# A hybrid layer's last attention pair: two pooling blocks in separate buffers, at other places of a hand-written order

## The chip, the cores and the metric

The kernel runs on one core of a Trainium2 chip. Its time is device microseconds of one execution. Five engines work side by side, each through its own queue in order: TensorE (PE: matmuls, with weight loads listed as PEld), VectorE (DVE), ScalarE (ACT), GpSimd (POOL) and SyncE (SP), which here issues the DMAs.

## What is computed

The reference is one layer over a sequence of 1024 rows of 1024 channels, in float32:

```
h = RMSNorm(x)
[pool_v | pool_gate | sb_q | sb_k | sb_v | sb_gate | mem_q | mem_gate] = h @ W_in
A (256 channels, 4 groups of 64): causal means over windows of 2, 4, 8, 16 rows, minus the row itself,
   times a 64x64 matrix per group, times a scale per channel
B (8 heads of 64): causal stick-breaking attention (sigmoid breaks, cumulative products, no softmax)
C (4 heads of 64): softmax attention into 256 memory tokens, with RMSNorm of q and k
each group's output * SiLU(its gate); concatenated @ W_out; + x
```

The change concerns group A. In the reference it is

```
csum  = cumsum(u) with a zero row ahead
means = (csum[t+1] - csum[max(t+1-w, 0)]) / count        # w = 2, 4, 8, 16 for the four groups
y     = einsum('bsgc,gcd->bsgd', stack(means) - u, pool_w) * pool_scale * SiLU(pool_gate)
```

## The kernel before

Activations lie with channels on the 128 partitions and the 1024 rows along the free axis. A float32 operand of a product is split into a high and a low part, and each product is three matmuls (high x high, high x low, low x high). A projection unit (`Unit`) makes 128 columns of `h @ W_in` for all rows: 16 steps of three matmuls, eight for the first 512 rows (th = 0) and eight for the rest, each half into one PSUM bank of the tag pj, of which there are two. Behind a half comes its `evac`: for a gate a sigmoid on ScalarE (L413) and a multiply on VectorE (L416), for a value of the pooling a copy on ScalarE (L893). Four quarters of the next unit's weights are split on ScalarE (L277) and GpSimd (L278) while a unit runs.

The attention of group B runs in four pairs of heads. Each pair has its q tiles in qa0, qb0 (even pairs) or qa1, qb1 (odd), its k tiles in KA0, KB0 or KA1, KB1, and its v tile in V0 or V1. The last pair, number 3, has the odd set. Its work goes in chunks: scores z on TensorE (L754), a sigmoid into a tile be on ScalarE (L760), a scan of up to 1024 elements on VectorE (L769); then, for one head of the pair, transposes on TensorE (ta, L593), a high part on ScalarE (L597) and a low part on VectorE (L598); for the other head a 32x32 transpose on VectorE (L771), a store to DRAM and a load back (zd; L779, L799 to L805), a high part on ScalarE (L824) and a low part on GpSimd (L825). Then come the products with v (av, L611), and their end on ScalarE (L630) and VectorE (L633, L634).

`weave` lays the attention's steps of a pair and a list of fill steps into one order, by planned TensorE times. For the last pair the fill is five units, 80 steps: u_pv[1], u_gp[1], u_gp[0], u_pv[0], u_gm[0] (the value and gate of pooling block 1, the gate and value of block 0, and a memory gate). The dictionary `places` puts further steps behind a fill step's number. `soon(us, fn)` puts work off until that much planned time has passed. In this part the order of all engines' instructions is the order of the program; behind `hand.close()` a planner orders VectorE, ScalarE, GpSimd and SyncE again, and may set transfers of the last part (`load_b`, L1228) earlier.

Group A is done by `pool_parts(r, gg)`, once for each block r of 128 channels (two groups of 64 channels). Its steps in order:

- `weights`: a memset on GpSimd (L902), two loads of pool_w by SyncE (L905), and later a split on ScalarE and GpSimd (L908, L909);
- `window_add(n, c)`: sums of two neighbours, then four, and so on, on VectorE (L927), 8 for block 1 and 4 for block 0, with short copies of the first columns on ScalarE (L931);
- `mean(h, c)`: four for each block, on VectorE (L941, L942 for the first 16 columns, L944), then, put off by 3.3 and 4.4 us of planned time, a high part ph on ScalarE (L949) and a low part pl on GpSimd (L952);
- `out_step(th)`: three matmuls into py (L969 to L971) and, soon after, the scale and the gate on VectorE (L974).

Both blocks use the same tiles: KA0 for the values and sums (us), V0 for pl, qa0 for the second sum (ps2), qb0 for ph, and the tag vt for the matrices (pw). Behind the 80 steps the second memory gate u_gm[1] runs (u_mg in the profile, as u_gm[0]), and then the output projection as seven block products in place of eight (oA, oS; L1274 to L1276) with operands of w_out loaded into qa0 with qb0, KA0, KB1.

Of the kernel before, what the change touches and what calls it, by code (L numbers as in the profile page):

```python
# [10 lines left out]
F32R = mybir.dt.float32r  # L11
# [5 lines left out]
P = 128  # L17
# [10 lines left out]
def layer_kernel(  # L28
# [17 lines left out]
    pool = ctx.enter_context(tc.tile_pool(name="pool", bufs=1))  # L46
# [9 lines left out]
    def f(ap):  # L56
        return ap.bitcast(F32)
# [3 lines left out]
    def ps(tag, name):  # L61
        return psum.tile([P, 512], F32, tag=tag, name=name, bufs=banks[tag])
# [9 lines left out]
    def slot(tag, name, dt=F32):  # L72
        return pool.tile([P, 1024], dt, tag=tag, name=name, bufs=bufs.get(tag, 1))

    def slot2(tag, name, dt=F32):
        return pool.tile([P, 2048], dt, tag=tag, name=name)
# [103 lines left out]
    def run(steps):  # L180
        for us, fn in steps:
            fn()
            tick(us)
# [23 lines left out]
    def tick(us):  # L207
        clock[0] += us
        while pending and pending[0][0] <= clock[0]:
            heapq.heappop(pending)[2].run()  # L210
# [5 lines left out]
    def weave(main, fill, keep=0, lag=0.0):  # L216
        span = sum(s.pe for s in main) + sum(c for c, _ in fill[: len(fill) - keep])
        total = sum(s.occ + s.pe for s in main)
        now, chain_end, gone, n = 0.0, lag, 0.0, 0
        ready = {}  # L220
        for s in main:
            at_ = max([span * gone / total] + [ready.get(k, 0.0) for k in s.needs])
            while n < len(fill) and now < at_:
                now += fill[n][0]
                fill[n][1]()
                tick(fill[n][0])
                n += 1
            s.fn()
            tick(s.pe)
            now = max(now, at_) + s.pe  # L230
            gone += s.occ + s.pe
            chain_end = max(chain_end, now) + s.occ
            for g in s.gives:
                ready[g] = chain_end + s.lat
        run(fill[n:])
# [50 lines left out]
    def chain(units, after=None):  # L286
        steps = []
        for n, u in enumerate(units):
            nxt = units[n + 1] if n + 1 < len(units) else after
            a = list(u.steps)  # L290
            if nxt is not None:
                a[0] = (KC, lambda f0=a[0][1], nxt=nxt: (f0(), nxt.load()))
                for i in range(4):
                    k = 7 + 2 * i
                    a[k] = (KC, lambda f0=a[k][1], nxt=nxt, i=i: (f0(), nxt.quarter(i)))
            steps += a
        return steps

    def lazy(make):
        box = []  # L300

        def get():
            if not box:
                box.append(make())
            return box[0]

        return get
# [577 lines left out]

    def pool_parts(r, gg):
        wbox = []
        get = lazy(lambda: slot2("KA0", f"us{r}"))
        pl_get = lazy(lambda: slot2("V0", f"pl{r}", dt=F32R)[:, 0:1024])
        box = []  # L890

        def evac(th, c, pt):
            nc.scalar.activation(get()[:, c], pt[:], AF.Copy)  # L893

        halves = (slice(0, 512), slice(512, 1024))

        def weights():
            t = pool.tile([P, 513], F32R, tag="vt", name=f"pw{r}")
            s2 = slot("qa0", f"ps2{r}")
            bw, bwr = s2[:, 896:1024], t[:, 0 : 2 * P].rearrange("p (n c) -> p n c", n=2)  # L900
            wbox.append(bwr)
            nc.gpsimd.memset(bw, 0.0)  # L902
            for h in range(2):
                rows = slice(h * HD, (h + 1) * HD)
                nc.sync.dma_start(bw[rows, rows], pool_w[0, 2 * r + h])  # L905

            def split():
                nc.scalar.activation(bwr[:, 0, :], bw, AF.Copy)  # L908
                nc.gpsimd.tensor_tensor(bwr[:, 1, :], bw, f(bwr[:, 0, :]), op=ALU.subtract)  # L909

            todo.append(soon(4.5, split))
            u, s = get()[:, 0:1024], get()[:, 1024:2048]
            box.extend([u, s, s2, slot("qb0", f"ph{r}", dt=F32R)])

        todo, heads = [], []

        def window_add(n, c):
            u, s, s2 = box[:3]
            if n == 1:
                todo[0].run()  # L920
            step = 1 << n
            prev, cur = (u if n == 0 else (s, s2)[(n - 1) % 2]), (s, s2)[n % 2]
            lo = HD if n == 2 * r + 1 else 0
            c0 = max(c.start, step)
            if c.start == 0 and n > 0:
                heads[-1].run()
            nc.vector.tensor_tensor(  # L927
                cur[lo:P, c0 : c.stop], prev[lo:P, c0 : c.stop], prev[lo:P, c0 - step : c.stop - step], op=ALU.add
            )
            if c.start == 0:  # L930
                heads.append(soon(2.0, lambda: nc.scalar.activation(cur[lo:P, 0:step], prev[lo:P, 0:step], AF.Copy)))  # L931

        def mean(h, c):
            (u, s, s2, ph), pl = box, pl_get()
            n = 2 * r + h
            heads[-1].run()
            rows = slice(h * HD, (h + 1) * HD)
            src, dst = (s, s2)[n % 2], (s, s2)[(n + 1) % 2]
            cn = cnt[rows, r * 16 : r * 16 + 16]
            if c.start == 0:  # L940
                nc.vector.tensor_tensor(dst[rows, 0:16], src[rows, 0:16], cn, op=ALU.mult)  # L941
                nc.vector.tensor_tensor(dst[rows, 0:16], dst[rows, 0:16], u[rows, 0:16], op=ALU.subtract)  # L942
            d = slice(max(16, c.start), c.stop)
            nc.vector.scalar_tensor_tensor(  # L944
                dst[rows, d], src[rows, d], cn[:, 15:16], u[rows, d], op0=ALU.mult, op1=ALU.subtract
            )

            def high():
                nc.scalar.activation(ph[rows, c], dst[rows, c], AF.Copy)  # L949

            def low():
                nc.gpsimd.tensor_tensor(pl[rows, c], dst[rows, c], f(ph[rows, c]), op=ALU.subtract)  # L952

            todo.append(soon(3.3, high))
            todo.append(soon(4.4, low))

        mix = [(0.0, weights)]
        mix += [(0.0, lambda n=n, c=c: window_add(n, c)) for n in range(2 * r + 2) for c in halves]
        mix += [(0.0, lambda h=h, c=c: mean(h, c)) for c in halves for h in range(2)]

        def out_step(th):
            ph, pl = box[3], pl_get()
            bwr = wbox[0]
            for it in todo:
                it.run()
            g = gg()
            c = slice(th * 512, (th + 1) * 512)
            pt = ps("pj", f"py{r}_{th}")
            nc.tensor.matmul(pt[:], bwr[:, 0, :], ph[:, c], start=True, stop=False)  # L969
            nc.tensor.matmul(pt[:], bwr[:, 0, :], pl[:, c], start=False, stop=False)  # L970
            nc.tensor.matmul(pt[:], bwr[:, 1, :], ph[:, c], start=False, stop=True)  # L971
            soon(
                0.5,
                lambda: nc.vector.scalar_tensor_tensor(  # L974
                    g[:, c], pt[:], gcol[:, 16 + r : 17 + r], g[:, c], op0=ALU.mult, op1=ALU.mult
                ),
            )

        return Unit(r * P, f"pv{r}", evac), mix + [(KC, lambda th=th: out_step(th)) for th in range(2)]
# [99 lines left out]
    u_q, u_k, u_v, u_g = [[sb[p][i][-1] for p in range(4)] for i in range(4)]  # L1079
# [84 lines left out]
    attn = sb_slots()  # L1164
# [3 lines left out]
    gp, u_gp = zip(*[gate_unit(256 + r * P, f"pg{r}", lambda r=r: gp_get()[:, r * 1024 : (r + 1) * 1024]) for r in range(2)])  # L1168
    gm, u_gm = zip(*[gate_unit(2816 + pr * P, f"mg{pr}", "be", lambda pr=pr: y_back[pr], (("pj", "pj"), ("tr", "av"))[pr]) for pr in range(2)])
    u_pv, po = zip(*[pool_parts(r, gp[r]) for r in range(2)])  # L1170
    weave(attn[2], chain([u_q[3], u_k[3], u_g[3], u_v[3]], u_pv[1]))
    units = chain([u_pv[1], u_gp[1], u_gp[0], u_pv[0], u_gm[0]], u_gm[1])

    places = {}
    for r, lo, hi, outs in ((1, 18, 46, (53, 57)), (0, 64.5, 77.5, (79.5, 79.7))):
        todo = po[r][:-2]
        for n, st in enumerate(todo):
            places.setdefault(int(lo + n * (hi - lo) / len(todo)), []).append(st)
        for at_, st in zip(outs, po[r][-2:]):
            places.setdefault(int(at_), []).append(st)  # L1180
# [213 lines left out]
```

## Time and profile before

| | |
|---|---|
| median of 3 runs | 527.57 us (525.86 to 528.05) |
| the profiled execution | 528.35 us, its span 526.2 us, mean clock 0.983 |
| TensorE busy | 499.3 us (95%) |
| VectorE busy | 403.4 us (77%) |
| ScalarE, GpSimd busy | 300.6 and 248.2 us |

The profile's times are from the span's start. A row of the timeline has start, length, engine, line, operation, output<-inputs by the program's names without numbers (so pv is u_pv[0] or u_pv[1]), and in brackets the idle time before it with what ended it. A row of the waits has who waited for whom, us in total, times, and the longest. A row of the table by stage has the stretch, its length, the busy time and number of instructions of each engine, the mean granted clock of TensorE (1.00 is full), the share of DMA and GB/s. The end of a matmul is modelled, so two matmuls overlap in the list; the time from start to start is what one occupies.

### The profile page before, as it was taken

To read this page: it belongs to the slowest core of one execution; us is meant where nothing else is said; L and a number is where in the kernel's file an instruction comes from. 1 tells how busy PE (TensorE), PEld (TensorE's weight loads), DVE (VectorE), ACT (ScalarE), POOL (GpSimd) and SP (SyncE) were. 2 spreads that over 40 slices of the span, in tenths; PEclk is the share of its full clock that TensorE was granted. 3 is DMA by queue.
4 is the path that set the end of the run, shared out by engine and by line. 5 is a ranking of instruction groups with operands and counts; after the bars stand their busy time and mean duration, and the time that the engine had idled before them with its cause. 6 is when DMAs were issued, how large, how long until landed. Compare 5 with 4: busy or idle time off the path is not lost.

```text
span 526.2 us, 7899 instructions
## 1 busy us (share of the span) xinstructions
PE 499.3 (95%) x2548; PEld 416.4 (79%) x2548; DVE 403.4 (77%) x621; ACT 300.6 (57%) x676; POOL 248.2 (47%) x239
## 2 busy tenths in 40 slices
PE   7889999999999999999999999997878969999997
PEld 6678888888888788888888888885767848888886
DVE  4777777877379975699665998499993469999973
ACT  6877757778348654676556665564463438462400
POOL 4580335355124453544735348462474772055791
PEclk9999999999999999999999999998989978999999
DMA  8911111533537744665755756635445217323123
GB/s 308 333 40 41 30 52 40 119 85 79 127 80 154 152 101 107 149 131 116 146 125 148 141 123 140 150 70 130 124 87 159 80 53 229 120 81 124 35 105 135
DMA packets 150080, 62.45 MB, mean 119 GB/s; under 512 B 104070, under 2 KB 139160, under 8 KB 150040
## 3 DMA queue, kind: packets, MB, share of 16 engines
q1 hardware_dynamic: 150040, 61.96, 45.9%
q8 instruction: 20, 0.33, 0.3%
q14 instruction: 20, 0.16, 0.1%
HBM read 40.97 MB, written 16.78 MB: 110 GB/s over the span
## 4 chain that ended last, share of the span: by engine, by line
PE 70%; DVE 11%; ACT 6%; issue 4%; POOL 4%; DMA 3%; SPq 1%; DVEq 0%; POOLq 0%; ACTq 0%
PE av L611 6%; PE u_q L254 6%; PE u_k L254 5%; PE u_g L254 5%; DVE be L769 5%; PE u_v L254 4%; PE z L754 4%; PE u_q L251 3%; PE oS L1274 3%; PE oS L1276 3%; PE oS L1275 3%; PE u_k L251 3%; PE u_g L251 2%; PE u_pv L254 2%; PE oA L1274 2%
## 5 line engine op out<-in xcount | busy, mean ns | idle before, releaser
L769 DVE TENSOR_TENSOR_SCAN be<-be,later 128x128 f32<-128x128 f32 (+3 forms) x64 | 97.8, 1533 | 15.0 <-ACT be L760 14.8
L825 POOL TENSOR_TENSOR al<-al,ah 128x512 fp32r<-128x512 f32 (+1 forms) x40 | 61.4, 1537 | 44.0 <-ACT ah L824 40.2
L760 ACT ACTIVATE be<-z 128x128 f32<-128x128 f32 (+3 forms) x96 | 47.0, 491 | 41.7 <-PE z L754 31.1
L611 PE MATMUL av<-al,V_v 128*128 128x256 f32 (+1 forms) x160 | 32.8, 287 | 8.0 <-DVE al L598 6.1
L597 ACT ACTIVATE ah<-ta 128x512 fp32r<-128x512 f32 (+1 forms) x40 | 22.2, 554 | 30.7 <-PE ta L593 22.9
L598 DVE TENSOR_TENSOR al<-ta,ah 128x512 fp32r<-128x512 f32 (+1 forms) x40 | 25.2, 630 | 17.1 <-ACT ah L597 15.4
L611 PEld LDWEIGHTS av<-ah,V_v 128*128 128x128 f32 x160 | 29.9, 190 | 8.5 <-PE z L754 1.0
L611 PEld LDWEIGHTS av<-al,V_v 128*128 128x128 f32 x160 | 24.6, 192 | 9.5 <-DVE al L598 7.4
L611 PE MATMUL av<-ah,V_v 128*128 128x256 f32 (+1 forms) x160 | 30.5, 272 | 0.9 <-PE z L754 0.6
L703 POOL TENSOR_SCALAR pe_m<-pe_m,nb_m 128x256 f32<-128x256 f32 x16 | 16.8, 1053 | 27.8 <-DVE nb_m L700 24.1
L630 ACT ACTIVATE avt<-av,ve_v 64x128 f32<-64x128 f32 x64 | 19.8, 357 | 17.6 <-PE av L611 9.5
L754 PE MATMUL z<-KA_k,qa_q 128*128 128x512 f32 (+3 forms) x96 | 25.7, 352 | 2.7 <-ACT be L760 2.7
L824 ACT ACTIVATE ah<-al 128x512 fp32r<-128x512 f32 (+1 forms) x40 | 23.4, 584 | 6.8 <-DMA al<-zd 3.8
L251 PE MATMUL u_g<-hh,wh_g 128*128 128x512 f32 x64 | 26.5, 415 | 0.0
L251 PE MATMUL u_v<-hh,wh_v 128*128 128x512 f32 x64 | 26.3, 411 | 0.0
L251 PE MATMUL u_k<-hh,wh_k 128*128 128x512 f32 x64 | 26.2, 410 | 0.0
L1274 PE MATMUL oS<-bs,hh 128*128 128x512 f32 (+1 forms) x68 | 25.9, 380 | 0.0
L1276 PE MATMUL oS<-bs,hl 128*128 128x512 f32 (+1 forms) x68 | 25.8, 379 | 0.0
L771 DVE STREAM_TRANSPOSE be<-be 128x128 f32<-128x128 f32 (+7 forms) x32 | 24.9, 779 | 1.1
L754 PE MATMUL z<-KB_k,qb_q 128*128 128x512 f32 (+3 forms) x96 | 25.7, 350 | 0.0
L1275 PE MATMUL oS<-bs,hh 128*128 128x512 f32 (+1 forms) x68 | 25.6, 377 | 0.0
L692 ACT ACTIVATE pe_m<-z_m,nb_m,qsc 128x256 f32<-128x256 f32 x32 | 17.8, 561 | 13.5 <-DVE nb_m L688 11.0
(322 smaller groups left out, 1579.1 us busy)
## 6 DMA issues: line engine op xcount, KB each, us to landing
al<-zd SPq DMA_DIRECT2D x24, 256.0 KB, 2.9
x<-in_x_dram SPq DMA_DIRECT2D x8, 512.0 KB, 6.2
wr_q<-in_w_in_dram SPq DMA_DIRECT2D x4, 512.0 KB, 3.7
wr_k<-in_w_in_dram SPq DMA_DIRECT2D x4, 512.0 KB, 4.8
wr_v<-in_w_in_dram SPq DMA_DIRECT2D x4, 512.0 KB, 3.9
KA_k<-KA_k SPq DMA_DIRECT2D x8, 256.0 KB, 3.5
KB_k<-KB_k SPq DMA_DIRECT2D x8, 256.0 KB, 3.7
wr_g<-in_w_in_dram SPq DMA_DIRECT2D x4, 512.0 KB, 3.8
```

What stands on the lines that cost most here:

```text
L251: nc.tensor.matmul(pt[:], wh[:, kc], hh[k][:, c], start=(k == 0), stop=False)
L254: nc.tensor.matmul(pt[:], w[:, kc], h[k][:, c], start=False, stop=(k == KD - 1 and n == 1))
L598: low = lambda: nc.vector.tensor_tensor(al[:, :w], tp[:, :w], f(ah[:, :w]), op=ALU.subtract)
L611: nc.tensor.matmul(av[:, 256 - bw : 256], vs[n], part[:, o : o + bw], start=(first and part is ah and n == 0), stop=(last and part is al a ...
L754: nc.tensor.matmul(zp[:, 0:w], q[h][:, tcol], k[h][:, m, s0 : s0 + w], start=(m == 0), stop=(m == 1))
L760: nc.scalar.activation(t[:, s0 : s0 + w], zp[:, 0:w], AF.Sigmoid, scale=-(HD**-0.5))
L769: nc.vector.tensor_tensor_scan(t[:, rev], t[:, rev], mask, 1.0, op0=ALU.mult, op1=ALU.max)
L771: nc.vector.transpose(t[:, 0:L], t[:, 0:L])
L825: nc.gpsimd.tensor_tensor(lo[:, 0:w], f(lo[:, 0:w]), f(hi[:, 0:w]), op=ALU.subtract)
L1274: nc.tensor.matmul(bk[:, c], xh[:, tcol], wh[:, c], start=(n == 0), stop=False)
L1275: nc.tensor.matmul(bk[:, c], xh[:, tcol], wl[:, c], start=False, stop=False)
L1276: nc.tensor.matmul(bk[:, c], xl[:, tcol], wh[:, c], start=False, stop=(n == 3))
```

## The change

The order of the five units becomes u_gp[1], u_pv[1], u_pv[0], u_gp[0], u_gm[0]. Block 1's pooling steps go from places 18 to 46 to places 32 to 56, its two products from 53 and 57 to 61 and 64. Block 0's go from 64.5 to 77.5 to places 53 to 68, its products from 79 to 74 and 77. Block 0 gets tiles of its own: V0 for the values and sums, KA1 for ph and pl, qb1 for the second sum, qa1 for the matrices. Block 1 keeps KA0, qa0, qb0 and vt, and its pl goes from V0 to KB1. The operations and their shapes stay.

```diff
     def pool_parts(r, gg):
         wbox = []
-        get = lazy(lambda: slot2("KA0", f"us{r}"))
-        pl_get = lazy(lambda: slot2("V0", f"pl{r}", dt=F32R)[:, 0:1024])
+        get = lazy(lambda: slot2(("V0", "KA0")[r], f"us{r}"))
+        pl_get = lazy(lambda: slot2("KB1", "pl1", dt=F32R)[:, 0:1024] if r else box[4])
         box = []
...
         def weights():
-            t = pool.tile([P, 513], F32R, tag="vt", name=f"pw{r}")
-            s2 = slot("qa0", f"ps2{r}")
+            if r:
+                t = pool.tile([P, 513], F32R, tag="vt", name=f"pw{r}")
+                s2, ph = slot("qa0", f"ps2{r}"), slot("qb0", f"ph{r}", dt=F32R)
+            else:
+                t = slot("qa1", f"pw{r}", dt=F32R)
+                both = slot2("KA1", f"ph{r}", dt=F32R)
+                s2, ph = slot("qb1", f"ps2{r}"), both[:, 0:1024]
...
-            box.extend([u, s, s2, slot("qb0", f"ph{r}", dt=F32R)])
+            box.extend([u, s, s2, ph] if r else [u, s, s2, ph, both[:, 1024:2048]])
...
-            (u, s, s2, ph), pl = box, pl_get()
+            (u, s, s2, ph), pl = box[:4], pl_get()
...
-    weave(attn[2], chain([u_q[3], u_k[3], u_g[3], u_v[3]], u_pv[1]))
-    units = chain([u_pv[1], u_gp[1], u_gp[0], u_pv[0], u_gm[0]], u_gm[1])
+    weave(attn[2], chain([u_q[3], u_k[3], u_g[3], u_v[3]], u_gp[1]))
+    units = chain([u_gp[1], u_pv[1], u_pv[0], u_gp[0], u_gm[0]], u_gm[1])
 
     places = {}
-    for r, lo, hi, outs in ((1, 18, 46, (53, 57)), (0, 64.5, 77.5, (79.5, 79.7))):
+    for r, lo, hi, outs in ((1, 32, 56, (61, 64)), (0, 53, 68, (74, 77))):
         todo = po[r][:-2]
```

## The prediction

> **What bounds the kernel now.** I read the page's first two parts, then tables by stage, then the waits of TensorE, and only then single instructions.
>
> ```profile
> PE 499.3 (95%) x2548; PEld 416.4 (79%) x2548; DVE 403.4 (77%) x621; ACT 300.6 (57%) x676; POOL 248.2 (47%) x239
> PE   7889999999999999999999999997878969999997
> DVE  4777777877379975699665998499993469999973
> PEclk9999999999999999999999999998989978999999
> ```
>
> TensorE is busy 95% of the span; its row drops below 9 in slices 28 to 31 and 33 of 13.2 us each (counting from 1), between 355 and 434 us, which is the last pair and what follows it. The clock row dips in the same place. In slices 27 to 30 VectorE is at 9, then at 3 and 4, then at 6 and 9. So the work that this change moves stands where VectorE is full, beside a stretch where it is not.
>
> The list of fill steps gives the stages. A fill step is three matmuls of one projection unit, 16 steps to a unit. The fourth unit (u_pv, steps 48 to 63) begins at 392.55, the fifth (u_mg, from step 64) at 411.18; counting L251 rows back from there, step 33 begins at 364.71 and step 20 at 342.2. From start to start a matmul of a unit takes 0.23 us (the last two rows), a step 0.7.
>
> ```profile
> 364.71 0.39 PE L251 MATMUL u_pg<-hh,wh_pg 128*128 128x512 f32 x1
> 389.07 0.63 PE L754 MATMUL z<-KA_k,qa_q 128*128 128x512 f32 x2
> 392.55 0.39 PE L251 MATMUL u_pv<-hh,wh_pv 128*128 128x512 f32 x1
> 411.18 0.39 PE L251 MATMUL u_mg<-hh,wh_mg 128*128 128x512 f32 x1
> 411.41 0.39 PE L254 MATMUL u_mg<-hl,wh_mg 128*128 128x512 f32 x1
> ```
>
> The table by stage (columns: length, then busy us and count of each engine, mean granted clock):
>
> ```profile
> core 0: us, PE busy (x) PEld busy (x) DVE busy (x) ACT busy (x) POOL busy (x), PEclk, DMA share, GB/s
> 342.20:364.70 22.50, 18.53 (x99) 15.06 (x98) 21.75 (x26) 12.34 (x33) 11.63 (x11) 1.00 0.43 92
> 364.70:392.50 27.80, 22.76 (x105) 18.59 (x104) 27.23 (x31) 14.94 (x35) 13.15 (x9) 0.88 0.55 119
> 392.50:411.10 18.60, 17.26 (x95) 14.50 (x95) 7.17 (x12) 7.46 (x17) 10.22 (x10) 1.00 0.41 128
> 411.10:424.20 13.10, 13.10 (x66) 10.73 (x64) 9.08 (x15) 6.21 (x16) 7.74 (x9) 1.00 0.20 58
> 424.20:432.20 8.00, 3.33 (x7) 1.85 (x7) 5.11 (x7) 2.48 (x4) 6.84 (x6) 0.65 0.16 48
> 432.20:445.50 13.30, 13.30 (x50) 10.63 (x49) 11.61 (x16) 9.65 (x17) 5.34 (x4) 0.83 0.77 250
> ```
>
> In the first two stages VectorE is the bound (49.0 of 50.3 us); in the next two TensorE; in the fifth neither: a chain. The waits of TensorE say which:
>
> ```profile
> PE av L611 <- DVE al L598: 5.1, 3, 3.5
> PE py L970 <- POOL pl L952: 3.3, 2, 2.0
> PE z L754 <- ACT be L760: 2.7, 3, 1.7
> PE av L611 <- POOL al L825: 1.7, 2, 1.3
> PE py L969 <- ACT ph L949: 1.3, 1, 1.3
> ```
>
> The first is VectorE's queue in the attention, the second and fifth are block 0 of the pooling, whose products stand right behind its means.
>
> **The change part by part.** I call the stages A (steps 20 to 32), B (33 to 47), C (48 to 63), D (64 to 79) and the tail behind it. The attention steps and the number of fill steps stay, so the matmul order stays but for unit names and the four groups of products. What moves on VectorE is the pooling (tile us) and the gates (tile gp):
>
> ```profile
> 342.20:364.70 22.50, 4.73 (x6) 0.59 (x3) 0.00 (x0) 1.00 0.43 92
> 364.70:392.50 27.80, 6.91 (x10) 0.83 (x2) 1.27 (x1) 0.88 0.55 119
> 411.10:424.20 13.10, 6.62 (x11) 0.98 (x3) 0.00 (x0) 1.00 0.20 58
> 424.20:432.20 8.00, 1.96 (x2) 1.25 (x2) 2.86 (x2) 0.65 0.16 48
> ```
>
> These four are tile us (length, then VectorE, ScalarE, GpSimd); the next three are tile gp, VectorE first.
>
> ```profile
> 342.20:364.70 22.50, 0.65 (x1) 1.20 (x2) 0.00 (x0) 1.00 0.43 92
> 364.70:392.50 27.80, 1.32 (x2) 0.61 (x2) 0.00 (x0) 0.88 0.55 119
> 392.50:411.10 18.60, 2.17 (x3) 0.59 (x1) 0.00 (x0) 1.00 0.41 128
> ```
>
> *Stage A.* Block 1's weights go from step 18 to 32 and its eight window adds from 20..35 to 33..46 (32 plus 24/13 per place). The gate of block 1 now comes first, so its multiplies (steps 7 and 15) leave the stage. VectorE keeps 21.75 - 4.73 - 0.65 = 16.4 us against 18.53 of TensorE: the stage becomes TensorE's, 22.5 to 18.5, a gain of **4.0** (bounds 2 and 4: a wait may remain where a long scan meets the short lookahead).
>
> *Stage B.* Out go the 6.91 of pooling and 1.32 of gates (block 0's gate unit moves to steps 48 to 63). In come all eight adds: 4.73 plus the two last of the old row, 1.59 and 0.69 (rows below), 7.0. VectorE has 27.23 - 6.91 - 1.32 + 7.0 = 26.0. TensorE at full clock would need about 22.76 - 27.8 x 0.12 = 19.4 (estimate, from the row). VectorE still bounds it: gain 27.8 - 26.0 = 1.8. The upper bound lets work slip past step 48, into the 4.6 us in which VectorE idles at 394.8: 6.4; the lower is 0, the same congestion. I take **2.0**, near the row's sum, since VectorE's queue is in order and the adds stand between the scans.
>
> ```profile
> 370.23 1.59 DVE L927 TENSOR_TENSOR ps<-us 64x504 f32<-64x504 f32 x1
> 375.77 0.69 DVE L927 TENSOR_TENSOR ps<-us 64x512 f32<-64x512 f32 x1
> 399.44 0.69 DVE L598 TENSOR_TENSOR al<-ta,ah 128x512 fp32r<-128x512 f32 x1 [4.61 <-ACT ah L597]
> 368.53 4.18 POOL L825 TENSOR_TENSOR al<-al,ah 128x512 fp32r<-128x512 f32 x2 [10.29 <-ACT ah L824]
> ```
>
> *Stage C.* VectorE keeps 7.17 - 2.17 = 5.0 and takes block 1's means (6.91 - 2.28 = 4.6), a gate multiply 0.7, block 0's four adds (4.0 of the 6.62), the first two of its means (2.6) and one product scaling 0.75: 17.7 us against 17.26 of TensorE, from 39% busy to full. Each subtraction of L598 may stand behind an add or a mean; the transposes run one chunk, about three fill steps of 0.7 us, ahead of the product that needs it, which hides 2 us. I charge **-1.5**; bounds 0 and -5, the latter the 5.1 us of such waits of the whole last pair. The wait for L825 (1.3 of the 1.7 above, at 396) stood behind GpSimd's splits for block 0's weights and block 1's lows, which now come later: **+1.3**. GpSimd gets block 1's four lows (1.3 us each, by the L952 row of the tail below) in steps 53 to 60, where it had 10.2 of 18.6 us: room. The second product group of block 1 (step 64) takes the bank of a gate half that ends at step 63, and so waits for a sigmoid (0.60, L413) and a multiply (0.66, L416), less one step of 0.7 us between them: **-0.6**, bounds 0 and -3.5 if the multiply is stuck in VectorE's queue.
>
> ```profile
> L413 ACT ACTIVATE gp<-u_pg x4: 598/600/603, 346.1 to 392.5; 128x512 f32<-128x512 f32 x4
> L416 DVE TENSOR_TENSOR gp<-u_pg,gp x4: 650/664/676, 347.4 to 394.2; 128x512 f32<-128x512 f32 x4
> ```
>
> *Stage D and the tail.* Block 0's products go from behind step 79 to behind 74 and 77, its last means to step 66. Today:
>
> ```profile
> 425.73 0.49 PE L969 MATMUL py<-ph,pw 128*128 128x512 f32 x1 [1.34 <-ACT ph L949]
> 428.19 0.79 PE L970 MATMUL py<-pl,pw 128*128 128x512 f32 x1 [1.97 <-POOL pl L952]
> 431.21 0.80 PE L970 MATMUL py<-pl,pw 128*128 128x512 f32 x1 [1.37 <-POOL pl L952]
> 432.23 0.63 PE L251 MATMUL u_mg<-hh,wh_mg 128*128 128x512 f32 x1
> 429.90 1.26 POOL L952 TENSOR_TENSOR pl<-us,ph 64x512 fp32r<-64x512 f32 x1
> ```
>
> The six products occupy 8.0 us; at 0.23 us from start to start they need 1.4. Gain **6.6**. Behind them the clock is low: u_mg takes 13.3 us for 16 steps that need 11.2 at 0.7: gain **2.1**. Both belong to the same gaps; the chain's cover is gone if the lows are late again. GpSimd then has, in D, its 7.74 us plus most of today's 6.84: some 14 of 14.5. So I charge **-0.5** (bounds 0 and -4.7, today's three waits together).
>
> *With one answer, at zero.* The other buffers: the last score product is issued at 389.07, ahead of step 45, and block 0 touches KA1, qa1 and qb1 only from step 53, block 1 KB1 from 48; nothing waits there. SyncE: four pool_w loads move with the weights; each waits for a memset on GpSimd, behind which loads of al queue, up to 3 chunks ahead of need. The four loads of w_out into KB1 leave the place at 374 where SyncE waited 7.8 us (row below) with an al load behind it; bounds 0 to +1. The first products' weights, in qa0 and qb0, come free earlier, but TensorE waits for none of them today, so zero.
>
> ```profile
> SPq L1228 <- PE z L754: 7.8, 1, 7.8
> ```
>
> The clock, by the trace: after the gaps of 1.34 to 1.97 us the fifth and sixth stage show 0.65 and 0.83. The Trainium skill ("TensorE: Matmul & The Clock Gate", Part 1) puts the drop to half clock after an idle window of about 3.4 us. By that rule alone these shorter gaps would cost no clock, and the sum would be smaller by 2.1; the trace has the low clock, and it decides.
>
> **Sum.** 4.0 + 2.0 - 1.5 + 1.3 - 0.6 + 6.6 + 2.1 - 0.5 = 13.4 us. The profiled execution took 528.35 us (span 526.2): 515.0. It lies 0.8 above the median, 527.57, so the median would be **514.2**. The upper ends of the gains (4 + 6.4 + 1.3 + 8.7 = 20.4) give 507.
>
> **The rivals.**
> 1. *VectorE still paces the last pair.* A and B lose or keep their waits, only the tail gains. For it: B's sum stays within 2 us of today's, C is now full too. Against it: A's slack of 2 us. Gain 8.7 - 0.5 - 1.5 + 1.3 = 8.0: about **520**.
> 2. *The products' waits only move.* Block 1's lows come from means at steps 48 to 54, and if VectorE lags by 5 us at step 48 (as much as it idles behind today), they land past step 61: TensorE waits as it does at 425, 8.7 us with the clock. Against it: seven steps, some 7 us, lie between the last mean and the first product. 13.4 - 8.7 = 4.7: **523**.
> 3. *Slower: the subtraction L598 behind the pooling.* Four transposed chunks fall in steps 52 to 60, where VectorE was idle 4.6 us at a stretch and is now full. If an add and a scan stand ahead of it, TensorE waits as long as its worst today, 3.5 us, and runs on at a low clock (B's 0.88 over 27.8 us is 3.3 us lost, behind two or three gaps): about 5 us in all. Four give 20: 527.6 - 13.4 + 20 - 1.5 (already charged) = **533**. From the third on it decides the sign. For it: the add beside GpSimd took 1.59 instead of 0.69 us (rows above: GpSimd's L825 was running), and more of both now coincide. Against it: the pooling's pieces are single instructions of 0.7 us with places two steps apart.
>
> The Trainium skill ("GPSIMD Engine Reference", Key points) says that GpSimd shares its SBUF interfaces with VectorE and that the two contend where a VectorE instruction has two SBUF inputs. The 1.59 us row agrees.
>
> **How the numbers follow.** The sum 0.58, rival 1 0.18, rival 2 0.10, rival 3 0.14. About 0.5% (2.6 us) is what a measurement of this kernel can tell from no change. Faster by more (below 524.9): 0.58 + 0.17 + 0.06 = 0.81. Within: 0.01 of rival 1, 0.04 of 2 and 0.02 of 3, 0.07. Slower: 0.12. The range from 507 (all upper ends) to 525 (beyond rival 2) leaves out 0.19. The forecast's own: 507 to 519.
>
> **What would show it.** A: TensorE's busy share at 1.0 up to step 32. B: VectorE near full, L598 still ending TensorE's waits. C: VectorE from 39% to over 85%, waits of a microsecond. Tail: no wait for L952 or L949 over 1 us, clock 1.00 in u_mg, its 16 steps in 11.2 us. The prediction is wrong if the products wait for pl at steps 61 or 74, if L598 waits in C add up to more than 5 us, or if the time from u_mg's first matmul to the end stays at 94 us.

## The result, and the profile after

The changed kernel takes 520.7 us in the median (518.4 to 526.5) against 527.8; the ratio is 0.9845 with an interval of 0.9811 to 0.9880. Timed again it gave 520.2 us and 0.9844 (0.9812 to 0.9877). It is faster by 1.6%, some 8 us, where 13.4 were forecast. The first profiled execution lost 4 us ahead of the last pair, which no edit touches, so the rows here are of the second, at 521.43 us (span 519.7), 6.9 below the profiled execution of before. The runs of the changed kernel lie in two groups, 517.2 to 519.2 us and 521.4 to 522.3, and both profiled executions (the first without its 4 us) belong to the longer one.

The page's rows of the changed kernel, 40 slices of 13.0 us:

```profile
span 519.7 us, 7909 instructions
PE   7889999999999999999999999998889599999997
DVE  4777777877469985599844999669999829999956
POOL 4580334365034452544745446463467581035692
```

Counted from 1, TensorE's dips in slices 28 to 31 are shallower (8, 8, 8, 9 for 7, 8, 7, 8) and the one in 33 is gone (9 for 6), but slice 32, which was full, is down to 5. VectorE's full stretch lies in slices 28 to 32 (9, 9, 9, 9, 8), where before it was 27 to 30 with 3 and 4 behind it; GpSimd's busiest slice of this part, 33, at 8, comes right behind the new dip. The table by stage, with A to D cut as in the prediction, then u_mg and the rest:

```profile
core 0: us, PE busy (x) PEld busy (x) DVE busy (x) ACT busy (x) POOL busy (x), PEclk, DMA share, GB/s
342.00:362.20 20.20, 18.00 (x102) 15.53 (x101) 17.08 (x20) 11.74 (x30) 10.07 (x10) 1.00 0.51 109
362.20:386.80 24.60, 20.66 (x103) 17.02 (x102) 24.24 (x25) 13.23 (x33) 12.45 (x8) 0.93 0.44 87
386.80:404.20 17.40, 16.57 (x91) 13.95 (x90) 16.58 (x26) 10.15 (x24) 13.71 (x13) 1.00 0.49 165
404.20:426.80 22.60, 16.84 (x74) 13.67 (x73) 12.88 (x16) 7.67 (x17) 15.59 (x14) 0.85 0.53 175
426.80:438.00 11.20, 11.20 (x49) 9.02 (x48) 8.86 (x13) 7.01 (x13) 3.57 (x4) 1.00 0.14 42
438.00:519.70 81.70, 77.86 (x349) 63.49 (x347) 70.58 (x104) 28.29 (x50) 36.84 (x24) 1.00 0.30 104
```

A, B and C went from 22.5, 27.8 and 18.6 us to 20.2, 24.6 and 17.4. D with the products was 13.1 + 8.0 and is 22.6. u_mg runs at full clock, 11.2 us for 13.3. TensorE's waits over the whole span, counterpart of the list of before (that list is of the last pair alone; there the first row is now 4.8 us, for 5.1):

```profile
PE av L611 <- DVE al L598: 5.8, 4, 3.0
PE py L974 <- DVE gp L416: 5.8, 1, 5.8
PE z L754 <- ACT be L760: 2.2, 1, 2.2
PE oA L1280 <- DVE bs L1249: 0.4, 1, 0.4
```

The waits of the products for ph and pl are gone (lines of the changed part stand five lower: L969 is L974, L952 is L957). In their place stands one wait of 5.8 us of the same products for the gate's multiply. VectorE, then the waiting matmul and GpSimd around it:

```profile
403.05 0.74 DVE L979 SCALAR_TENSOR_TENSOR gp<-py,gcol,gp 128x512 f32<-128x512 f32 x1
403.70 0.16 DVE L946 TENSOR_TENSOR ps<-us,cnt 64x16 f32<-64x16 f32 x1
403.89 0.62 DVE L947 TENSOR_TENSOR ps<-ps,us 64x16 f32<-64x16 f32 x1
404.44 1.81 DVE L949 SCALAR_TENSOR_TENSOR ps<-us,cnt 64x496 f32<-64x496 f32 x1
406.28 1.13 DVE L946 TENSOR_TENSOR us<-ps,cnt 64x16 f32<-64x16 f32 x1
407.44 1.19 DVE L947 TENSOR_TENSOR us<-us 64x16 f32<-64x16 f32 x1
408.55 0.73 DVE L949 SCALAR_TENSOR_TENSOR us<-ps,cnt,us 64x496 f32<-64x496 f32 x1
409.31 0.42 DVE L633 TENSOR_TENSOR av<-av,avt 64x256 f32<-64x256 f32 x1
409.77 0.41 DVE L634 TENSOR_TENSOR g_g<-g_g,av 64x256 f32<-64x256 f32 x1
410.11 0.68 DVE L416 TENSOR_TENSOR gp<-u_pg,gp 128x512 f32<-128x512 f32 x1
410.84 0.79 PE L974 MATMUL py<-ph,pw 128*128 128x512 f32 x1 [5.76 <-DVE gp L416]
404.22 0.40 PE L251 MATMUL u_mg<-hh,wh_mg 128*128 128x512 f32 x1
403.75 0.73 POOL L278 TENSOR_TENSOR wl_mg<-wr_mg,wh_mg 128x256 fp32r<-128x256 f32 x1
404.44 2.93 POOL L825 TENSOR_TENSOR al<-al,ah 128x512 fp32r<-128x512 f32 x2
407.34 1.25 POOL L957 TENSOR_TENSOR ph<-ps,ph 64x512 fp32r<-64x512 f32 x1
```

Fill step 64 is the u_mg matmul at 404.22; the product group behind it should follow at 404.9. It takes the bank of the gate half that ended with step 63, and the multiply that empties that bank stands in VectorE's queue behind two means of block 0 (L946 to L949), which take 5.6 us, and two short steps of the attention (L633, L634).

### The profile page after: what moved, and what is told of

It is laid out like the page before. It is cut to its first block, busy times and chain, and to the rows that moved or that the text cites. A ratio compares the mean times of both kernels' runs of the same rounds, so it can differ in the third digit from the quotient of the medians.

```text
span 524.7 us, 7909 instructions
## 1 busy us (share of the span) xinstructions
PE 498.8 (95%) x2548; PEld 417.3 (80%) x2548; DVE 405.2 (77%) x621; ACT 299.1 (57%) x676; POOL 246.7 (47%) x239
## 4 chain that ended last, share of the span: by engine, by line
PE 66%; DVE 16%; issue 6%; ACT 5%; POOL 5%; DMA 1%; SPq 0%; DVEq 0%; POOLq 0%; ACTq 0%
PE u_q L254 6%; PE av L611 5%; PE u_k L254 5%; DVE be L769 5%; PE u_g L254 5%; PE u_v L254 4%; PE z L754 4%; PE u_q L251 3%; PE oS L1279 3%; PE oS L1281 3%; PE oS L1280 3%; PE u_k L251 3%; PE u_g L251 2%; PE u_v L251 2%; PE u_mq L254 2%
## 5 line engine op out<-in xcount | busy, mean ns | idle before, releaser
L769 DVE TENSOR_TENSOR_SCAN be<-be,later 128x128 f32<-128x128 f32 (+3 forms) x64 | 95.8, 1501 | 15.6 <-ACT be L760 15.3
L825 POOL TENSOR_TENSOR al<-al,ah 128x512 fp32r<-128x512 f32 (+1 forms) x40 | 62.0, 1553 | 50.0 <-ACT ah L824 45.4
L760 ACT ACTIVATE be<-z 128x128 f32<-128x128 f32 (+3 forms) x96 | 47.1, 491 | 38.7 <-PE z L754 29.3
L598 DVE TENSOR_TENSOR al<-ta,ah 128x512 fp32r<-128x512 f32 (+1 forms) x40 | 25.2, 630 | 10.2 <-ACT ah L597 8.6
L824 ACT ACTIVATE ah<-al 128x512 fp32r<-128x512 f32 (+1 forms) x40 | 23.4, 584 | 16.0 <-PE av L611 7.7
L611 PEld LDWEIGHTS av<-al,V_v 128*128 128x128 f32 x160 | 24.6, 192 | 7.2 <-DVE al L598 7.0
L703 POOL TENSOR_SCALAR pe_m<-pe_m,nb_m 128x256 f32<-128x256 f32 x16 | 16.8, 1053 | 27.8 <-DVE nb_m L700 24.0
L254 PE MATMUL u_k<-hl,wh_k 128*128 128x512 f32 x64 | 25.3, 395 | 0.0
```

What stands on the lines that cost most here:

```text
L254: nc.tensor.matmul(pt[:], w[:, kc], h[k][:, c], start=False, stop=(k == KD - 1 and n == 1))
L598: low = lambda: nc.vector.tensor_tensor(al[:, :w], tp[:, :w], f(ah[:, :w]), op=ALU.subtract)
L611: nc.tensor.matmul(av[:, 256 - bw : 256], vs[n], part[:, o : o + bw], start=(first and part is ah and n == 0), stop=(last and part is al a ...
L760: nc.scalar.activation(t[:, s0 : s0 + w], zp[:, 0:w], AF.Sigmoid, scale=-(HD**-0.5))
L769: nc.vector.tensor_tensor_scan(t[:, rev], t[:, rev], mask, 1.0, op0=ALU.mult, op1=ALU.max)
L825: nc.gpsimd.tensor_tensor(lo[:, 0:w], f(lo[:, 0:w]), f(hi[:, 0:w]), op=ALU.subtract)
```

## The experiments

The table has the stages of the profiled execution of each kernel, from the first matmul of a fill step to that of the next stage (D to the first of u_mg; the last column is from there to the end), and the ratio to the kernel before.

| kernel | A | B | C | A to C | D | to the end | median us | ratio (interval) |
|---|---|---|---|---|---|---|---|---|
| before | 22.4 | 27.8 | 18.6 | 68.9 | 21.1 | 94.0 | 527.8 | |
| changed, again | 20.2 | 24.6 | 17.4 | 62.2 | 22.6 | 92.9 | 520.2 | 0.984 (0.981 to 0.988) |
| late_product | 21.5 | 20.7 | 20.5 | 62.7 | 17.0 | 92.1 | 515.7 | 0.980 (0.976 to 0.984) |
| other_bank | 21.7 | 20.7 | 20.5 | 62.9 | 15.8 | 93.6 | 516.9 | 0.980 (0.976 to 0.983) |
| block0_late | 21.9 | 22.5 | 18.6 | 62.9 | 23.4 | 93.6 | 523.7 | 0.992 (0.990 to 0.994) |
| buffers_only | 22.4 | 27.4 | 18.5 | 68.3 | 22.5 | 93.9 | 528.6 | 1.002 (1.001 to 1.003) |
| block1_early | 24.8 | 24.8 | 18.3 | 67.8 | 22.1 | 92.5 | 525.8 | 0.996 (0.994 to 0.997) |
| early_adds | 24.6 | 20.8 | 18.0 | 63.4 | 16.5 | 92.2 | 515.8 | 0.977 (0.974 to 0.980) |
| no_adds | 20.0 | 20.2 | 17.0 | 57.2 | 21.3 | 92.6 | 515.9 | 0.977 (0.975 to 0.979) |
| pool_adds | 25.2 | 23.0 | 17.1 | 65.3 | 17.0 | 92.2 | 518.9 | 0.982 (0.981 to 0.984) |
| block0_mid | 19.9 | 24.6 | 16.4 | 60.8 | 16.8 | 95.2 | 516.4 | 0.978 (0.976 to 0.979) |

### after_again

> The changed kernel once more. Theory: about 519 us, 0.984 of the kernel before, and block 1's second product group waits 4 to 6 us for the multiply L416, with the low clock behind it. Rival: the wait belonged to that one execution; then under 1 us here, and the time the same.

As the theory has it: the wait of 5.76 us is there in both profiled executions. No other execution of this kernel was profiled.

### late_product

```diff
-    for r, lo, hi, outs in ((1, 32, 56, (61, 64)), (0, 53, 68, (74, 77))):
+    for r, lo, hi, outs in ((1, 32, 56, (61, 67)), (0, 53, 68, (74, 77))):
```

> One number changed: block 1's second product group stands behind fill step 67 in place of 64. Theory (the group takes the bank of gate half pg0 th1, whose multiply is queued on VectorE behind block 0's means): the wait of 5.8 us goes, and 2 us of low clock with it; block 0's products may wait up to 2 us. 511 to 515 us, 0.970 to 0.977 of the kernel before. Rival (VectorE itself is the bound of this stretch, and another matmul waits for it): the wait comes back at step 67, at the next gate half or at block 0's products, and the time is within 2 us of the changed kernel's.

It measured 515.7 us in the median (four runs at 515.2 to 515.9, two at 520.3 and 520.6), 4.5 below the changed kernel timed beside it. By the two ratios it is 2.3, and their intervals overlap, so the gain in time is less sure than that in the trace, where D falls from 22.6 to 17.0. TensorE's waits over the whole span and the row of D:

```profile
PE av L611 <- DVE al L598: 5.2, 6, 2.0
PE z L754 <- ACT be L760: 1.9, 1, 1.9
PE av L611 <- POOL al L825: 1.8, 2, 1.1
PE py L974 <- DVE gp L416: 0.2, 1, 0.2
404.60:421.60 17.00, 15.69 (x75) 12.58 (x74) 10.77 (x17) 7.42 (x17) 15.33 (x14) 1.00 0.70 234
```

The wait for the multiply is down to 0.2 us and the clock of D is 1.00 for 0.85. What remains in D is a wait of 1.1 for L825: GpSimd is busy 15.3 of 17.0 us there. The time is 0.7 above the theory's bound; within 2 us of the changed kernel's, as the rival has it, it is neither by the medians nor, narrowly, by the ratios.

### other_bank

```diff
-            pt = ps("pj", f"py{r}_{th}")
+            pt = ps("tr" if r and th else "pj", f"py{r}_{th}")
```

> The changed kernel with every place kept; block 1's second product group alone goes into a bank of the tag tr, which no gate half uses. Theory (the wait is for the bank alone): the group at step 64 starts at once, the wait of 5.8 us for the multiply L416 goes with its low clock, although VectorE has the same order of work: 512 to 516 us, as late_product. Rival (VectorE's lag is the bound): the wait appears at the next user of a pj bank, the half of u_mg at step 72, or at block 0's products, and the time is 518 or more.

This separates the bank from the place: the order of TensorE and VectorE is that of the changed kernel. First TensorE, then the start and the end of the two means with the multiply, and GpSimd beside them:

```profile
404.67 0.39 PE L251 MATMUL u_mg<-hh,wh_mg 128*128 128x512 f32 x1
405.37 0.39 PE L974 MATMUL py<-ph,pw 128*128 128x512 f32 x1
404.16 0.71 DVE L946 TENSOR_TENSOR ps<-us,cnt 64x16 f32<-64x16 f32 x1
406.05 0.73 DVE L949 SCALAR_TENSOR_TENSOR us<-ps,cnt,us 64x496 f32<-64x496 f32 x1
407.61 0.68 DVE L416 TENSOR_TENSOR gp<-u_pg,gp 128x512 f32<-128x512 f32 x1
406.20 1.74 POOL L825 TENSOR_TENSOR al<-al,ah 128x512 fp32r<-128x512 f32 x1 [1.36 <-ACT ah L824]
```

The group starts 0.7 us behind step 64, at 405.37, though the multiply L416 ends only at 408.29; no later matmul of D waits for VectorE in its stead, and D is 15.8 us. The rival falls: VectorE's lag by itself was no bound there, the bank was. That the wait is for the bank is shown by this run. Its 516.9 us is 0.9 above the theory's range.

It shows a second thing. The same two means, in the same order, take 2.6 us here (404.16 to 406.78) for 5.6 above: GpSimd is idle for 1.36 us before 406.20, in the midst of them. With the bank of the changed kernel the group would have waited here from 405.37 to 408.29, about 2.9 us (an estimate from these rows). So the 5.8 us is the wait's size in the two profiled executions, not a fixed one.

### block0_late

```diff
-    for r, lo, hi, outs in ((1, 32, 56, (61, 64)), (0, 53, 68, (74, 77))):
+    for r, lo, hi, outs in ((1, 32, 56, (61, 64)), (0, 64.5, 77.5, (79.5, 79.7))):
```

> The changed kernel with block 0's pooling steps and products at the places they had before (64.5 to 77.5, products behind 79). Theory: with block 0's adds and means behind the gate half's multiply, the wait of block 1's second product group falls below 1.5 us, while the six matmuls in front of u_mg again take 7 to 8 us and u_mg runs at a low clock: 519 to 522 us, 0 to 3 above the changed kernel. Rival (the wait for the bank comes from the attention's work on VectorE): it stays at 5 us and the time is 525 or more.

```profile
PE py L975 <- POOL ph L957: 3.2, 2, 2.0
PE py L974 <- ACT ph L954: 1.8, 1, 1.8
PE py L974 <- DVE g_mg L416: 0.6, 1, 0.6
PE py L974 <- DVE gp L416: 0.3, 1, 0.3
```

Without block 0's adds and means ahead of it the multiply is in time (0.3 us) although the product stands behind 64, and the old chain at the end is back (3.2 + 1.8; the six products take 8.0 us, and the clock in u_mg is 0.88). So it was block 0's work, of which the two means stand directly ahead of the multiply in the rows above, and not the attention's, that held the bank. The mechanism is as expected; at 523.7 us the kernel is 2 us slower than the theory's range.

### buffers_only

Order and places as before; block 0's values in KB1, its other tiles as in the change; block 1's pl in V0.

> The kernel before with separate buffers alone: block 0 in KB1 (values and sums), KA1, qb1 and qa1, block 1 with its pl in V0; order of units and all places as before. Theory: no wait of the kernel before was for these buffers, so within 1.5 us of it (526 to 529). Rival (the earlier loads of w_out or SyncE's wait of 7.8 us counted): 2 to 4 us faster.

528.6 us, 0.2% above before: the buffers gain nothing by themselves. That the overlap needs them is argued from the program; no run has the new places with the old buffers.

### block1_early

late_product with the units in the order u_pv[1], u_gp[1], u_pv[0], u_gp[0], u_gm[0], block 1's list over 18 to 46, and the buffers of buffers_only.

> late_product with block 1's value unit first again and its adds and means at the old places 18 to 43; products at 61 and 67, block 0 as in late_product. Block 0's values are in KB1, block 1's pl in V0. Theory (stages A to C gain 6 to 7 us by moving block 1's vector work behind step 32): those stages go from 62.7 us back to 67 to 69 and the time to 519 to 522. Rival (the gain of these stages comes from the gate units and the rest of the change): 514 to 517.

A to C take 67.8 us, inside the 67 to 69 of the theory: the gain of these stages comes from where block 1's vector work stands. (The units are in the old order for block 1 here too, but early_adds below has that order as well and keeps 63.4 us.) The time is 4 us above what was expected, and D has it:

```profile
423.13 0.69 PE L611 MATMUL av<-al,V_v 128*128 128x256 f32 x2 [4.20 <-POOL al L825]
419.14 2.98 POOL L1255 TENSOR_TENSOR b_V<-g_g 128x512 f32<-128x512 f32 x2
422.09 0.98 POOL L825 TENSOR_TENSOR al<-al,ah 128x384 fp32r<-128x384 f32 x1
```

The planner set two subtractions of the output projection (L1255) into GpSimd's order ahead of the last low part of the attention. The likely reason is that V0, which they write, comes free earlier with this kernel's buffers; no run tests that.

### early_adds

```diff
+    steps_at = {1: (8, 16, 17, 18, 19, 20, 21, 22, 23, 46, 48, 50, 52), 0: (53, 54, 56, 58, 59, 61, 63, 64, 66)}
```

> late_product with block 1's value unit first again, its weights at step 8 and its eight adds at 16 to 23, where VectorE idles for some 7 us between 335 and 350 us; its means at 46 to 52 and all else as late_product. Theory (VectorE's queue bounds steps 25 to 60, and adds in front of it are free): stages B and C lose 4 to 6 us of late_product's 41 us: 509 to 513 us. Rival (the waits of those stages come from the scans and the buffers of be, not from the pooling): within 1.5 us of late_product, 514 to 517.

The rival was right on the time, 515.8 us, and neither on the cause. B and C lose 2.4 us, and A takes 3.1 more:

```profile
342.23 2.54 DVE L932 TENSOR_TENSOR ps<-us 128x510 f32<-128x510 f32 x2 [0.80 <-ACT us L936]
346.97 1.59 DVE L932 TENSOR_TENSOR ps<-us 64x504 f32<-64x504 f32 x1
357.33 0.52 DVE L598 TENSOR_TENSOR al<-ta,ah 128x384 fp32r<-128x384 f32 x1
357.91 0.45 PE L611 MATMUL av<-al,V_v 128*128 128x256 f32 x2 [3.48 <-DVE al L598]
```

VectorE's idle time in front of its full stretch could not take 5.5 us of adds: some take about twice their 0.6 to 0.7 us, the scans behind them start late (the one of 128x384 at 348.57 for 345.63 in late_product), and L598 at 357 meets a queue that no longer drains before it.

### no_adds

```diff
         def window_add(n, c):
...
+            if r:
+                return
```

> late_product without block 1's eight window adds: its means are taken from the values themselves, so groups 2 and 3 of the pooling come out other than the reference; 7 us of VectorE's work and four short copies of ScalarE are left out. Theory (VectorE's queue bounds stages A to C, 62.7 us, of which TensorE needs about 55): they fall to 56 to 58 us and the time to 509 to 511. Rival (the scans and the buffers of be bound these stages by themselves): above 61 us, and 514 to 516.

```profile
382.30:399.30 17.00, 16.54 (x91) 13.90 (x90) 15.71 (x24) 9.83 (x23) 12.05 (x13) 1.00 0.50 164
407.21 0.80 PE L977 MATMUL py<-ph,pw 128*128 128x512 f32 x1 [4.40 <-DVE gp L416]
```

A to C fall to 57.2 us, in the theory's range: 7 us of VectorE's work out, 5.5 us of time gained, so VectorE's queue does bound these stages by about that much. But the kernel is not faster than late_product: TensorE, early now, waits 4.4 us for the same multiply at step 67. The expectation for the time left out the next bound.

### pool_adds

early_adds with L932 of block 1 on GpSimd.

> early_adds with block 1's eight adds on GpSimd in place of VectorE. Theory (VectorE bounds, GpSimd has room in stage A): A falls from 24.6 to 20 to 22 us and the time to 511 to 514. Rival (adds on GpSimd, 1.3 us each, lengthen VectorE's instructions beside them and hold up the splits L278 and the low parts L825 in GpSimd's queue): 516 to 520, with waits for L825 of 2 us or more.

```profile
353.27 0.80 PE L611 MATMUL av<-al,V_v 128*128 128x256 f32 x2 [3.60 <-POOL al L825]
```

The rival: 518.9 us, and A is the longest of all.

### block0_mid

```diff
+    steps_at = {1: (32, 33, 35, 37, 39, 41, 43, 44, 46, 48, 50, 52, 54), 0: (53, 56, 58, 61, 63, 65, 66, 67, 68)}
+    for r, outs in ((1, (61, 67)), (0, (76, 79))):
```

> late_product with block 0's adds at 56, 58, 61 and 63, its means at 65 to 68 and its products behind 76 and 79. Theory (VectorE is full in stage C and has 6 us free in D): C loses 1.5 to 2.5 us of 20.5, the lows just come in time: 513 to 514.5. Rival (block 0's lows come late in GpSimd's queue): its products wait 1 to 3 us at 76 to 79, and the time is 515 to 517.

A to C fall by 1.9 us against late_product (A is 1.6 shorter, B 3.9 longer, C 4.1 shorter) and no product of the pooling waits for a low part, yet it takes 516.4 us. The loss is behind u_mg:

```profile
PE oA L1281 <- DVE bs L1250: 1.4, 2, 1.2
PE oA L1280 <- ACT bs L1249: 1.1, 1, 1.1
```

The first products of the output projection wait for their weights' splits, which neither theory had. Why the planner's order came out so is not tested.

The best versions run that compute the reference are late_product and early_adds, at 515.7 and 515.8 us; their difference is no result.

## Why the prediction was right, and where it was wrong

The direction, the mechanisms and the range (507 to 525) held; the gain was half to two thirds of the sum.

- **A to C.** Forecast 4.0 + 2.0 - 1.5 + 1.3 = 5.8 us, measured 68.9 - 62.2 = 6.7; 0.7 of that is a product group that stood in C and now stands in D, so 6.0. Block1_early shows the cause by undoing it, no_adds the bound by taking work away. The split differs: A gave 2.2 for 4.0, B 3.3 for 2.0, C 1.2 (0.5 without the group) for -0.2. It is not fixed either: late_product, with the same order up to step 64, gave 0.9, 7.2 and -1.9. A's average (VectorE 16.4 of 18.5 us) hid that VectorE idles at the stage's start, 2.22 us at 345.7 for one scan, and is nearly full from 349.5 on; the wait of 2.2 us for L760 at its end was in the bounds.
- **The bank at step 64: the step that failed.** The prediction had the wait, its place and its reason, sized it as -0.6 us and bounded it at -3.5. In the profiled executions it is 5.8 us, with a low clock behind it (0.85 over D). D there is 22.6 - 17.0 = 5.6 us longer than late_product's, in which a wait of 1.1 for L825 has come instead. The sizing took the multiply's own 0.66 us and the sigmoid's 0.60; the queue ahead of it was not counted out, though the text had VectorE full in C and two means at 61 and 63. Those means were priced undisturbed, 2.6 us for two; they took 5.6, with GpSimd's L278, L825 and L957 beside them. Where GpSimd was idle in their midst (other_bank) they took the 2.6, and the wait would have been about 2.9, inside the bounds. So by this estimate the queue of VectorE makes up about half of the 5.8 and GpSimd beside it the other half, which the prediction had for the adds (its third rival) and not for this term. Between kernels the step is worth less than 5.6: late_product gains 2.3 us by the ratios, 4.5 by the medians.
- **D and the tail.** With the bank out of the way (late_product) D is 17.0 for 21.1 us and holds one product group more, 0.7: 4.8 of the forecast 6.6 - 0.5 = 6.1. Most of the difference is the wait for L825 in GpSimd's full queue, 1.1, charged as 0.5 on the lows. The clock in u_mg: 13.3 to 11.2, the forecast 2.1. Behind u_mg the output projection takes 81.7 us for 80.7, a loss that the prediction did not have; 0.4 of it is the wait of oA for L1249, the rest is not explained.
- **At zero.** The buffers: right, by buffers_only. What the planner sets into the queues of the output projection is not zero in other versions: 4.2 us in block1_early, 2.5 in block0_mid.
- **The rivals.** Rival 1 (VectorE still paces) holds as a description of B; its time, 520, is the measured one, but by another cause, since A to C gained their full sum. Rival 2 was the failing step's neighbour: a product's wait moved to step 64, for a bank and not for a low part. Rival 3 did not happen: waits for L598 are 5.8 us against 6.1 over the whole span.

With the forecast's other terms kept and this one at 5.6, the sum is 13.4 + 0.6 - 5.6 = 8.4 us; the two profiled executions differ by 6.9. Between them lie 0.9 more in A to C, 2.0 less in D (4.1 for 6.1, the product group of 0.7 included), 1.0 lost behind u_mg, and some 0.7 gained ahead of A and outside the span. That 8.4 is near the 7 to 8 of the medians is in part luck.

## What to carry to other kernels

Where a step is put between two users of rotating banks, price the release of the bank it will get by the whole queue ahead of the releasing instruction, not by that instruction alone, and ask which GpSimd instructions will run beside that queue: two means took 2.6 us or 5.6. A bank of another tag, or three steps later, took 5.6 to 6.8 us out of the traced stage and 2 to 4.5 out of the time. Work taken from an engine that bounds a stage pays only up to the next wait: no_adds took 5.5 us out of three stages and gave 4.4 of it back at one bank. An average over a stage does not show that an engine idles at its beginning and is full at its end; cut the stage where the queue fills.

## What was not expected of the hardware

VectorE's smallest instructions suffer most beside GpSimd: the 64x16 operations take about 0.17 us undisturbed and 0.62, 1.13 and 1.19 us in the rows at 403.89, 406.28 and 407.44 above. Each of the three began while an instruction of GpSimd ran, and ended 0.03 to 0.04 us behind the end of one: at 404.51 behind L278 (404.48), at 407.41 behind the second L825 (407.37), at 408.63 behind L957 (408.59). So what these three lose is what was left of GpSimd's instruction; in no_adds, where one began at 402.59 beside a first and ended at 404.99 behind a second (L825, 403.71 to 404.97), it took 2.40 us. The Trainium skill ("GPSIMD Engine Reference", Key points) names the shared interfaces for VectorE instructions with two SBUF inputs; these rows agree.

The clock after a short gap is not the same each time. In the changed kernel a wait of 2.20 us at 359.95 left the clock of A at 1.00; in late_product, with the same order up to there, one of 1.91 at 359.60 left 0.92:

```profile
359.95 0.50 PE L754 MATMUL z<-KA_k,qa_q 128*128 128x256 f32 x2 [2.20 <-ACT be L760]
359.60 0.77 PE L754 MATMUL z<-KA_k,qa_q 128*128 128x256 f32 x2 [1.91 <-ACT be L760]
342.00:363.50 21.50, 19.59 (x103) 16.90 (x102) 18.59 (x23) 12.59 (x32) 10.05 (x9) 0.92 0.51 111
```

The first row is the changed kernel's, the others late_product's. The length of the wait does not decide it: other_bank waited 2.19 us there and has 0.92 as well, the first profiled execution of the changed kernel 1.90 and has 1.00. In late_product the low stretch is 359.7 to 363.1, at a clock of 0.50, and B has 1.00; the changed kernel has such a stretch in B instead, 379.9 to 383.3. With it B and C change places too (24.6 and 17.4 against 20.7 and 20.5), with the sum of A to C within 0.5 us. What decides it stays open.
